# A decoder block on one Trainium2 core: the bias table read backwards, the input rows loaded before a key weight, and the row factors made one projection earlier

## The chip, the cores and the metric

The kernel is one program on one core of one Trainium2 chip. The metric is the device time of one execution in microseconds (us). TensorE (PE in the rows) multiplies, VectorE (DVE), ScalarE (ACT) and GpSimd (POOL) work on tiles, SyncE (SP) issues the transfers. PEld is TensorE's loading of weights, which overlaps its products.

## The reference

One decoder block for x of 512 tokens by 1024 channels in float32, with one batch and one layer:

```
h = rms_norm(x)
q, k, v (three branches), gates, conv inputs = h @ w_in
NSA heads (8 query heads, 2 key groups, width 64):
    logit[t, s] = q[t] . k[s] / 8 + bias[head, bucket(t - s)], causal
    branches: compressed keys (31 blocks), selected blocks, window; each softmax, gated, summed
conv heads: y = b * dwconv3(c * x~)
x1 = x + rms_norm(concat @ w_out)
y  = x1 + rms_norm(gated conv MLP(rms_norm(x1)))
```

The bias depends on the distance t - s alone, so each head has one vector of 512 numbers, and every row of the table is that vector shifted by one place.

## The kernel before

Every dense product is made of three passes in a short float32 form: each operand is split into hi and lo. For a weight tile ScalarE rounds hi (L84) and VectorE subtracts to get lo (L85); for eight weights, those of the compression's first layer (c1_0 to c1_7, shown as w_c_0 to w_c_7 in the lists below), GpSimd makes lo instead, on the same line 85. A product of a weight with h is three matmuls for each of eight k steps, 24 in all, on lines 167 (hi by hi), 168 and 169 (lo of the weight), so the lo part is first needed by the third.

Weights come through one object W, in the order of use: 512 KB each, loaded some tiles ahead into three raw buffers (L72) and split fewer tiles ahead. All transfers are issued by SP in the order of the program.

The start runs in this order on TensorE: the products of the value columns (pv, L297 to L299), then k0 and k1 (the keys of the selected and of the window branch, pp_k), c0 (the keys to compress, pp_c), q0 and q1 (queries), then c1 (the values to compress) together with the first attention part. ScalarE takes the mean square of the four row tiles of x (L307, tile xt); GpSimd makes 1/rms of it (L308, L309); VectorE puts it on a diagonal (dgs), and one product of ones and dgs (prb, L335) spreads it over the partitions; ScalarE copies it to Rb (L336). Every projection that leaves PSUM is multiplied by Rb on VectorE (L372: kt for keys, ct for what is compressed, qt for queries). Keys are then split into KK (L131, L132), queries into Q (hi L397, lo L398). ScalarE also writes the values V (L350).

What is to be compressed is laid out by `blocks`: eight additions for the keys' tile and eight for the values' tile (L417, tile x), then a split into X (L131, L132), which the first compression layer multiplies (`hidden_steps`, ph, L441).

Attention goes in parts of four heads. For each head two products make the logits (sc, L593); one VectorE instruction adds the bias table and takes the minimum of the row (L597); ScalarE takes the exponential (L599); `scale` divides by the row sums two heads at a time (L604, L606; then head 0 on GpSimd, L611, the others on ScalarE, L613). The probabilities are transposed on TensorE (tr, L622), split (pth, ptl) and multiplied with the values (o, L630, L631). Between these pieces the order of work named in ORDER fills TensorE: c1, then q2, the compression's hidden layer, q3, and the convolution heads' weights from g0 on (pcg).

The bias table U[p, h, u] holds, at row p, the vector of head h shifted by p. The vector goes to DRAM (vd, 8 by 640), is copied there 128 times (two transfers to vrows, one for four heads each), and is read back with a pitch that is one number short of the row, so that each row is shifted by one more place.

From the end of the startup on, the order on each engine is found by a scheduler, which follows the program's order but may move an instruction past others.

Of the kernel before, what the change touches and what calls it, by code (L numbers as in the profile page):

```python
"""Hybrid decoder block (NSA heads + short convolution, then a gated conv MLP) on one core.

Float32 products run as three float32r passes over operands split exactly into
hi + lo (12 + 12 significant bits): hi*hi + hi*lo + lo*hi.  The attention logits
and the P.V products keep all four parts.

With these shapes N_SEL covers every key block (n_sel = SEQ / L_SLC) and WINDOW =
SEQ, so the selected and the sliding branch both see exactly the causal keys: top-k
only permutes the blocks, and softmax does not depend on their order.
"""  # L10
# [11 lines left out]
F32 = mybir.dt.float32  # L22
# [8 lines left out]
NT = S // P          # token tiles  # L31
KT = D // P          # contraction tiles of the model width
# [9 lines left out]
# the projections and the first layer of the compression as they fill the gaps of the attention:  # L42
# values to compress c1, queries q, hidden layer h, second layer s, then gate g, input x, output gate b
ORDER = ("c1 q2:4 h0 q2:4 h1 q3:4 h2 q3:4 h3 g0:4 h4 g0:4 h5 x0:4 h6 x0:4 h7 s b0 "
         "g1 x1 b1 g2 x2 b2 g3 x3 b3")
LOADS = "T0 g w T1 T2 w b T3 T4 T5 w T6 T7", "x0 x1 v x2 x3 s0", "s1"
T_TILES = 20         # kc vc ks kw q0-3 then (c x b) x 4
WARM = 8             # products on zeros while the first loads are under way
# [6 lines left out]
class Stream:  # L55
    """The dense weights in the order of their use: loaded some tiles ahead, split fewer ahead."""

    def __init__(self, tc, nc, raw, ring, items, loads=3, splits=2):
        self.tc, self.nc, self.raw, self.ring, self.items = tc, nc, raw, ring, items
        self.loads, self.splits = loads, splits  # L60
        self.raws, self.tiles = [], []
        self.at = 0
        self.early = False     # whether the splits go before what was emitted shortly before them
        self.pool_lo = set()  # tiles whose lo part GpSimd makes
        self.pieces = {}     # tiles that are split in pieces of so many columns
        self.other = {}      # tiles that go to another pool than the ring
# [41 lines left out]
def block_kernel(ctx: ExitStack, tc: tile.TileContext, a, out):  # L108
# [20 lines left out]
    def split(hi, lo, src):  # L129
        """hi = src rounded to 12 significant bits, lo = src - hi (exact)."""  # L130
        act(hi, src, AF.Copy)  # L131
        nc.vector.tensor_tensor(lo, src, f32(hi), op=ALU.subtract)  # L132

    VK = [0, 2, 5, KT]       # the k tiles of the value columns, as they share a tile of the ring
# [27 lines left out]
    W = Stream(tc, nc, rawp, ringp, items)  # L162
# [30 lines left out]
    # the tensor engine's clock comes up while the first loads are under way  # L193
# [6 lines left out]
    # bias tables: U[p, h, u] = -(bias of distance p + 384 - u), +BIG where it is negative  # L200
    # row r of vrows is the whole of vd; reading with a pitch one short shifts it by r
# [4 lines left out]
    vrows = [dram.tile([P, 4 * 640], F32, name=f"vrows{n}") for n in range(2)]  # L206

    def load(what):
        """A name of LOADS: w the next weights, g the gains, b and v the bias (its table, then its vector),
        s rows of shifted bias, T columns and x rows of the input."""  # L210
        if what == "w":
            W.ahead(0, len(W.raws) + 1)
        elif what == "g":
            nc.sync.dma_start(gT, a["g_mix_pre"])
        elif what == "b":
            nc.sync.dma_start(oh[:NB, :S], a["onehot"])
            nc.sync.dma_start(relT, a["relT"])
        elif what == "v":
            nc.sync.dma_start(vd[:, :S], vec[:NH, :S])
            nc.sync.dma_start(vd[:, S:], vbig)  # L220
        elif what[0] == "s":
            n = int(what[1])
            nc.sync.dma_start(vrows[n], bass.AP(tensor=vd.tensor, offset=vd.offset + n * 4 * 640,
                                                ap=[[0, P], [1, 4 * 640]]))
        elif what[0] == "T":
            k = int(what[1])
            nc.sync.dma_start(xT[:, k, :], a["xT"][k * P:(k + 1) * P, :])
        else:
            t = int(what[1])
            nc.sync.dma_start(xt[:, t, :], a["x"][t * P:(t + 1) * P, :])  # L230
# [17 lines left out]
    def rstd_of(ss, name):  # L248
        """1 / rms of a row from the two halves of its mean square."""
        r = const.tile([P, 1], F32, tag="rstd", bufs=4, name=name)  # L250
        nc.gpsimd.tensor_scalar(r, ss[:, 0:1], ss[:, 1:2], EPS, op0=ALU.add, op1=ALU.add)  # L251
        nc.gpsimd.tensor_tensor(r, r, mhalf, op=ALU.pow)
        return r
# [17 lines left out]
    # The mean square of a row divides what comes out of the products, not what goes in.  # L271
    R = const.tile([P, 2, NT], F32, name="R")        # 1 / rms and its negative, by token
    Rb = ph1.tile([P, S], F32, name="Rb")            # the same, by token along the row
# [28 lines left out]
    for what in LOADS[2].split():  # L302
        load(what)

# [13 lines left out]
    def proj(name, ahead=None):  # L318
        p = mm_bank(f"pp_{name}")
        for _ in proj_steps(p, W.next(ahead)):  # L320
            pass
        return p

    W.ahead(2, 3)
    for t in range(NT):
        square1(t)
    W.ahead(3, 3)
    pk = [proj("k0", 0), proj("k1", 0)]
    pc0 = pt_bank("pp_c0")
    wq = W.next(0)  # L330
    W.ahead(1, 2)
    for _ in proj_steps(pc0, wq, 0, 3):
        pass
# [3 lines left out]
    for _ in proj_steps(pc0, wq, 3, KT):  # L337
        pass
    nc.vector.tensor_scalar(R[:, 1], R[:, 0], -1.0, None, op0=ALU.mult)
    U = r16("U").rearrange("p (h u) -> p h u", h=NH)  # L340
    for n, v in enumerate(vrows):
        nc.sync.dma_start(U[:, 4 * n:4 * n + 4, :], bass.AP(tensor=v.tensor, offset=v.offset + P - 1,
                                                            ap=[[4 * 640 - 1, P], [640, 4], [1, S]]))
# [44 lines left out]
    # queries, scaled by -1/8; even heads keep hi in the low half, odd heads in the high half  # L388
# [14 lines left out]
    # X[(l parity, d), l // 2, k/v, hi/lo, (group, block)] = kv + pe, the blocks padded to 32  # L403
# [25 lines left out]
    def hidden_steps(c):  # L429
        """First layer of the compression; rows 0-63 from X hi, rows 64-127 from X lo."""  # L430
        if c == 0:
            phs[0] = mm_bank("ph")
        w = W.next()
        for l in range(2):
            l2 = 2 * c + l
            for kv in range(2):
                xs = X[:, l2, kv].rearrange("p s g n -> p (s g n)")
                for s in range(2):
                    cc = slice(l * 512 + kv * 256, l * 512 + kv * 256 + 256)
                    # one group over the bank: its first product opens it  # L440
                    MM(phs[0][:, kv * 256:kv * 256 + 256], xs, w[:, s, cc],  # L441
                       start=l2 == 0 and kv == 0 and s == 0, stop=l2 == 15 and kv == 1 and s == 1)
            yield

    def second_layer():
        w2 = ph1.tile([P, 2, 2, HD], F32, tag="gz", bufs=1, name="w2")     # (half, k/v)
# [103 lines left out]
    def compressed_softmax(i):  # L550
# [7 lines left out]
        uv = U[:, :, u0:u0 + 16 * (nv - 1) + 1:16]  # L558
# [15 lines left out]
    class Part:  # L574
        """Four heads of a group on a tile of queries: one branch, or both for the first tile."""
# [8 lines left out]
        def score(self, r):  # L584
# [9 lines left out]
            for b in range(len(self.bs)):  # L594
                v = p[:, b * nk:(b + 1) * nk]
                m = self.mins[:, r, b:b + 1]
                nc.vector.tensor_tensor_reduce(v, sc[:, b * nk:(b + 1) * nk], U[:, h, 384 - P * i:S], 1.0, 3e38,  # L597
# [54 lines left out]
    def finish(o, i, g):  # L652
        # rows 0-63: V hi . P, rows 64-127: V lo . P
# [23 lines left out]
    for n, (i, g, bs) in enumerate(parts):  # L677
# [6 lines left out]
        # the share that goes between this part's pieces  # L684
# [45 lines left out]
    def token_major(w_tiles, ys, acts, on_half, on_tile, order):  # L730
        """The last products of a streamed contraction, one token tile after another."""
# [14 lines left out]
    with tc.tile_pool(name="ph2", bufs=1, reuse_waits="tile") as ph2:  # L746
# [49 lines left out]
        # the first tiles of the MLP in halves of the tokens, behind the norm of the last rows  # L796
# [83 lines left out]
def _bucket_onehot():  # L880
    """[bucket, 511 - distance], a constant of the shapes alone."""
# [5 lines left out]
    m[bucket, S - 1 - d] = 1.0  # L887
# [50 lines left out]
```

## Time and profile before

| what | value |
| --- | --- |
| time, median of 3 runs | 634.92 us (633.7 to 635.61) |
| span of the profiled execution | 633.9 us |
| TensorE busy | 617.5 us, 97% |
| VectorE busy | 382.2 us, 60% |
| ScalarE busy | 306.5 us, 48% |
| GpSimd busy | 62.7 us, 10% |
| mean granted TensorE clock | 0.995 |

The times are of whole executions, and the span is from the first to the last instruction of the one execution that was profiled, whose own time the page doesn't give: the median lies 1.0 us above that span, and the three runs lie within 1.9 us of each other. A row of a timeline gives the start, the duration, the engine, the line, and the tiles; `x4` joins four like instructions, and what stands in brackets is the idle time of the engine just before, with what ended it. Durations of matmuls overlap, so the pace of TensorE is read from the starts.

### The profile page before, as it was taken

The numbers are of one execution on the slowest core, as the hardware profiler recorded it, in microseconds if no ns is written. First come the engines' busy times: TensorE is split into PE (matmuls) and PEld (weight loads), VectorE is DVE, ScalarE is ACT, GpSimd is POOL, SyncE is SP. The second block draws the span as 40 slices with busy tenths as digits, with TensorE's granted clock in tenths as the row PEclk, the third lists the DMA queues.
The fourth block names the chain that finished last, engine by engine and source line by source line (L and its number), as shares of the span: only waits on it lengthen the run. The fifth ranks groups of instructions, "written<-read, shape, count | busy, mean of one in ns | idle before, by whom it ended". The sixth has DMA issues, their size and how long they took to land.

```text
span 633.9 us, 8027 instructions
## 1 busy us (share of the span) xinstructions
PE 617.5 (97%) x2980; PEld 511.3 (81%) x2980; DVE 382.2 (60%) x668; ACT 306.5 (48%) x556; POOL 62.7 (10%) x88
## 2 busy tenths in 40 slices
PE   8998899999999999999999999999999999999995
PEld 6886688887778788898888888888888888888884
DVE  5379967898988756648666656565656542222225
ACT  6546765798878644426443434444344422222212
POOL 1102453002130202200000000000000000000001
PEclk9999899999999999999999999999999999999999
DMA  8993355201121483004222233232322232232203
GB/s 293 329 304 129 133 180 189 74 10 43 42 78 53 169 280 130 8 5 143 93 96 98 99 100 101 100 100 99 101 87 95 89 114 87 94 100 99 67 0 133
DMA packets 25302, 72.00 MB, mean 114 GB/s; under 512 B 3136, under 2 KB 7048, under 8 KB 25008
## 3 DMA queue, kind: packets, MB, share of 16 engines
q1 hardware_dynamic: 25264, 71.50, 33.9%
q8 instruction: 23, 0.38, 0.2%
q14 instruction: 15, 0.12, 0.1%
HBM read 67.50 MB, written 4.74 MB: 114 GB/s over the span
## 4 chain that ended last, share of the span: by engine, by line
PE 80%; DVE 10%; DMA 3%; ACT 3%; issue 2%; POOL 1%; SPq 0%; DVEq 0%; POOLq 0%; ACTq 0%
PE pu L168 13%; PE pu L169 13%; PE pu L167 13%; PE z L743 6%; PE z L742 6%; PE z L744 6%; PE y L744 2%; PE y L743 2%; PE y L742 2%; DVE x L417 2%; DMA raw_q<-in_w_t 2%; PE tr L622 2%; PE sc L593 2%; PE o L631 1%; PE o L630 1%
## 5 line engine op out<-in xcount | busy, mean ns | idle before, releaser
L167 PE MATMUL pu<-h2T,w_u 128*128 128x512 f32 (+1 forms) x384 | 142.8, 372 | 0.0
L168 PE MATMUL pu<-h2T,w_u 128*128 128x512 f32 (+1 forms) x384 | 142.7, 372 | 0.0
L169 PE MATMUL pu<-h2T,w_u 128*128 128x512 f32 (+1 forms) x384 | 142.6, 371 | 0.0
L167 PEld LDWEIGHTS pu<-h2T,w_u 128*128 128x128 f32 x384 | 72.3, 188 | 12.6
L168 PEld LDWEIGHTS pu<-h2T,w_u 128*128 128x128 f32 x384 | 72.3, 188 | 12.6 <-DVE h2T L132 0.2
L169 PEld LDWEIGHTS pu<-h2T,w_u 128*128 128x128 f32 x384 | 72.3, 188 | 12.4
L826 DVE SCALAR_TENSOR_TENSOR cv<-pu,ffnw,cv 128x511 f32<-128x511 f32 x44 | 32.9, 749 | 70.2 <-ACT cv L825 70.2
L85 DVE TENSOR_TENSOR w_d<-raw_d,w_d 128x1024 fp32r<-128x1024 f32 x22 | 26.9, 1224 | 72.8 <-ACT w_d L84 72.8
L742 PE MATMUL z<-w_d,aT 128*128 128x512 f32 x176 | 68.5, 389 | 0.0
L743 PE MATMUL z<-w_d,aT 128*128 128x512 f32 x176 | 68.5, 389 | 0.0
L744 PE MATMUL z<-w_d,aT 128*128 128x512 f32 x176 | 68.5, 389 | 0.0
L825 ACT ACTIVATE cv<-pu,ffnw 128x512 f32<-128x512 f32 x44 | 30.3, 688 | 64.0 <-PE pu L169 63.9
L84 ACT ACTIVATE w_d<-raw_d 128x1024 fp32r<-128x1024 f32 x22 | 23.3, 1059 | 75.2 <-PE z L744 75.2
L85 DVE TENSOR_TENSOR w_u<-raw_u,w_u 128x1024 fp32r<-128x1024 f32 x44 | 53.4, 1217 | 5.9 <-ACT w_u L84 5.8
L84 ACT ACTIVATE w_u<-raw_u 128x1024 fp32r<-128x1024 f32 x44 | 46.2, 1052 | 6.6 <-PE pu L169 6.3
L599 ACT ACTIVATE P<-P,mins 128x512 f32<-128x512 f32 (+3 forms) x64 | 35.4, 554 | 11.5 <-DVE mins L597 11.1
L742 PEld LDWEIGHTS z<-w_d,aT 128*128 128x128 f32 x176 | 33.0, 188 | 6.9
L744 PEld LDWEIGHTS z<-w_d,aT 128*128 128x128 f32 x176 | 33.0, 188 | 6.9
L743 PEld LDWEIGHTS z<-w_d,aT 128*128 128x128 f32 x176 | 33.0, 188 | 6.7
L131 ACT ACTIVATE aT<-cv 128x512 fp32r<-128x512 f32 x22 | 13.9, 632 | 49.5 <-DVE cv L843 49.5
L251 POOL TENSOR_SCALAR rsz<-ssz 128x1 f32<-128x1 f32 x4 | 1.2, 300 | 355.2 <-ACT jz L865 355.2
L827 DVE SCALAR_TENSOR_TENSOR cv<-pu,ffnw,cv 128x510 f32<-128x510 f32 x44 | 32.8, 748 | 1.5
(215 smaller groups left out, 1158.7 us busy)
## 6 DMA issues: line engine op xcount, KB each, us to landing
raw_u<-in_w_u SPq DMA_DIRECT2D x44, 512.0 KB, 3.3
raw_d<-in_w_d SPq DMA_DIRECT2D x22, 512.0 KB, 3.2
raw_c<-in_w_c SPq DMA_DIRECT2D x8, 512.0 KB, 3.3
raw_o<-in_w_o SPq DMA_DIRECT2D x8, 512.0 KB, 3.4
vrows<-vd SPq DMA_DIRECT2D x2, 1280.0 KB, 10.4
xT<-in_xT SPq DMA_DIRECT2D x8, 256.0 KB, 5.3
xt<-in_x SPq DMA_DIRECT2D x4, 512.0 KB, 7.1
raw_q<-in_w_t SPq DMA_DIRECT2D x4, 512.0 KB, 7.0
```

The costliest lines, as they stand in the source:

```text
L84: self.nc.scalar.activation(t[:, 0, cs], self.raws[n][:, cs], AF.Copy)
L85: eng.tensor_tensor(t[:, 1, cs], self.raws[n][:, cs], f32(t[:, 0, cs]), op=ALU.subtract)
L167: MM(dst, wh, xh, start=first, stop=False)
L168: MM(dst, wh, xl, start=False, stop=False)
L169: MM(dst, wl, xh, start=False, stop=last)
L599: act(v, v, AF.Exp, bias=m, scale=-1.0, accum_out=self.sums[:, r, b:b + 1])
L742: MM(y, oh_, w[:, 0, cs], start=first, stop=False)
L743: MM(y, ol_, w[:, 0, cs], start=False, stop=False)
L744: MM(y, oh_, w[:, 1, cs], start=False, stop=last)
L825: act(t, pu, AF.Copy, scale=ffnw[:, m, 2:3])
L826: nc.vector.scalar_tensor_tensor(t[:, 1:], pu[:, :S - 1], ffnw[:, m, 1:2], t[:, 1:], op0=ALU.mult, op1=ALU.add)
L827: nc.vector.scalar_tensor_tensor(t[:, 2:], pu[:, :S - 2], ffnw[:, m, 0:1], t[:, 2:], op0=ALU.mult, op1=ALU.add)
```

## The change

Four edits, all in the first part of the kernel.

- The two copies to vrows are gone. The vector is written the other way round in distance, at place 127 of a row of vd, with 127 large numbers ahead of it; UR is read from vd with a pitch of one number, and the attention reads each of its rows backwards (`bias`, step -1, and step -16 for the compressed branch).
- The four row tiles of x (and the vector between them) are loaded before the second key weight k1; after them follow k1, c0 and q0.
- ScalarE's order follows from that: the squares of x stand ahead of the split of k1.
- prb and Rb are made after three of the eight k steps of k1, where they were made after three of c0's.

```diff
-LOADS = "T0 g w T1 T2 w b T3 T4 T5 w T6 T7", "x0 x1 v x2 x3 s0", "s1"
+LOADS = "T0 g w T1 T2 w b T3 T4 T5 w T6 T7 w", "x0 x1 v x2 x3 w"
...
-    W = Stream(tc, nc, rawp, ringp, items)
+    W = Stream(tc, nc, rawp, ringp, items, loads=0)
...
-            nc.sync.dma_start(vd[:, :S], vec[:NH, :S])
-            nc.sync.dma_start(vd[:, S:], vbig)
-        elif what[0] == "s":
-            n = int(what[1])
-            nc.sync.dma_start(vrows[n], bass.AP(tensor=vd.tensor, offset=vd.offset + n * 4 * 640,
-                                                ap=[[0, P], [1, 4 * 640]]))
+            nc.sync.dma_start(vd[:, P - 1:P - 1 + S], vec[:NH, :S])
+            nc.sync.dma_start(vd[:, :P - 1], vbig[:, :P - 1])
...
-    W.ahead(2, 3)
     for t in range(NT):
         square1(t)
-    W.ahead(3, 3)
-    pk = [proj("k0", 0), proj("k1", 0)]
-    pc0 = pt_bank("pp_c0")
+    W.ahead(3, 4)
+    pk = [proj("k0", 0), mm_bank("pp_k1")]
     wq = W.next(0)
-    W.ahead(1, 2)
-    for _ in proj_steps(pc0, wq, 0, 3):
+    for _ in proj_steps(pk[1], wq, 0, 3):
         pass
     prb = mm_bank("prb")
     MM(prb, ones, dgs, start=True, stop=True)
     act(Rb, prb, AF.Copy)
-    for _ in proj_steps(pc0, wq, 3, KT):
+    for _ in proj_steps(pk[1], wq, 3, KT):
+        pass
+    pc0 = pt_bank("pp_c0")
+    W.loads = 3
+    wq = W.next(0)
+    W.ahead(1, 2)
+    for _ in proj_steps(pc0, wq):
         pass
     nc.vector.tensor_scalar(R[:, 1], R[:, 0], -1.0, None, op0=ALU.mult)
-    U = r16("U").rearrange("p (h u) -> p h u", h=NH)
-    for n, v in enumerate(vrows):
-        nc.sync.dma_start(U[:, 4 * n:4 * n + 4, :], bass.AP(tensor=v.tensor, offset=v.offset + P - 1,
-                                                            ap=[[4 * 640 - 1, P], [640, 4], [1, S]]))
+    UR = r16("UR").rearrange("p (h u) -> p h u", h=NH)
+    for n in range(2):
+        nc.sync.dma_start(UR[:, 4 * n:4 * n + 4, :], bass.AP(tensor=vd.tensor, offset=vd.offset + n * 4 * 640,
+                                                             ap=[[1, P], [640, 4], [1, S]]))
+
+    def bias(h, u, n, step=1):
+
+        v = UR[:, h, S - 1 - u]
+        return bass.AP(tensor=v.tensor, offset=v.offset, ap=[*v.ap, [-step, n]])
...
-        uv = U[:, :, u0:u0 + 16 * (nv - 1) + 1:16]
+        uv = bias(slice(None), u0, nv, 16)
...
-                nc.vector.tensor_tensor_reduce(v, sc[:, b * nk:(b + 1) * nk], U[:, h, 384 - P * i:S], 1.0, 3e38,
+                nc.vector.tensor_tensor_reduce(v, sc[:, b * nk:(b + 1) * nk], bias(h, 384 - P * i, nk), 1.0, 3e38,
...
-    m[bucket, S - 1 - d] = 1.0
+    m[bucket, d] = 1.0
```

The lists below are the instructions of one engine in program order, without durations; lines of the changed kernel differ by a few. The number of matmuls is the same.

On ScalarE, before, from the split of k1 (the first row) to the split of c0 (the last), with the squares (xt, L307) and the values (V, L350) between them:

```order
L84 ACTIVATE w_k_292<-raw_k_190 128x1024
L307 ACTIVATE xt,ss_295<-xt 128x1024
L350 ACTIVATE V_139<-pv_144,R 128x4x64
L307 ACTIVATE xt,ss_300<-xt 128x1024
L350 ACTIVATE V_139<-pv_145,R 128x4x64
L307 ACTIVATE xt,ss_305<-xt 128x1024
L350 ACTIVATE V_139<-pv_146,R 128x4x64
L307 ACTIVATE xt,ss_310<-xt 128x1024
L350 ACTIVATE V_139<-pv_147,R 128x4x64
L84 ACTIVATE w_c_315<-raw_c_245 128x1024
```

The same place of the changed kernel, to the copy of Rb:

```order
L299 ACTIVATE xt,ss_290<-xt 128x1024
L299 ACTIVATE xt,ss_295<-xt 128x1024
L351 ACTIVATE V_139<-pv_144,R 128x4x64
L351 ACTIVATE V_139<-pv_145,R 128x4x64
L299 ACTIVATE xt,ss_300<-xt 128x1024
L351 ACTIVATE V_139<-pv_146,R 128x4x64
L299 ACTIVATE xt,ss_305<-xt 128x1024
L351 ACTIVATE V_139<-pv_147,R 128x4x64
L84 ACTIVATE w_k_310<-raw_k_209 128x1024
L84 ACTIVATE w_c_313<-raw_c_211 128x1024
L325 ACTIVATE Rb<-prb 128x512
```

The split of k1 has moved from ahead of the four squares to behind the last of the values, and Rb follows the split of c0 directly.

On VectorE, before, at the second half of the first attention part (the row minima L597, the row sums, and the additions x of the values to compress):

```order
L597 ISA P_585,mins_561<-sc_584,U 128x512
L597 ISA mins_561 128x1
L604 RECIPROCAL sums_560<-sums_560 128x2
L606 TENSOR_TENSOR sums_560<-sums_560,G 128x2
L85 TENSOR_TENSOR w_q_523<-raw_q_486,w_q_523 128x1024
L372 TENSOR_TENSOR ct_626<-pp_c_596,Rb 128x512
L597 ISA P_662,mins_595<-sc_661,U 128x512
L597 ISA mins_595 128x1
L417 TENSOR_TENSOR x_1_0_628<-ct_626,peT 64x8x31 x2
L604 RECIPROCAL sums_560<-sums_560 128x2
L417 TENSOR_TENSOR x_1_0_628<-ct_626,peT 64x8x31
L606 TENSOR_TENSOR sums_560<-sums_560,G 128x2
```

In the changed kernel the first attention part on VectorE, from the lo of the first two queries' heads on:

```order
L399 SCALAR_TENSOR_TENSOR Q_456<-qt_512,Q_456 64x512 x2
L85 TENSOR_TENSOR w_q_519<-raw_q_482,w_q_519 128x1024
L373 TENSOR_TENSOR qt_548<-pp_q_518,Rb 128x512
L598 ISA P_559,mins_557<-sc_558,UR 128x512
L598 ISA mins_557 128x1
L598 ISA P_565,mins_557<-sc_564,UR 128x512
L598 ISA mins_557 128x1
L399 SCALAR_TENSOR_TENSOR Q_456<-qt_548,Q_456 64x512 x2
...
L605 RECIPROCAL sums_556<-sums_556 128x2
L607 TENSOR_TENSOR sums_556<-sums_556,G 128x2
L373 TENSOR_TENSOR ct_622<-pp_c_592,Rb 128x512
L418 TENSOR_TENSOR x_1_0_624<-ct_622,peT 64x8x31 x2
```

Both pairs of row sums now stand ahead of ct and of the additions x. The lo of the second queries (qt_548) stands behind two row minima; before, both queries were split before the first of them.

On GpSimd, before, behind the last 1/rms:

```order
L611 TENSOR_SCALAR P_563<-P_563,sums_560 128x512
L85 TENSOR_TENSOR w_c_0_597<-raw_c_0_488,w_c_0_597 128x1024
L85 TENSOR_TENSOR w_c_1_643<-raw_c_1_490,w_c_1_643 128x1024
L85 TENSOR_TENSOR w_c_2_727<-raw_c_2_600,w_c_2_727 128x1024
L611 TENSOR_SCALAR P_662<-P_662,sums_594 128x512
```

and in the changed kernel:

```order
L85 TENSOR_TENSOR w_c_0_593<-raw_c_0_484,w_c_0_593 128x1024
L85 TENSOR_TENSOR w_c_1_639<-raw_c_1_486,w_c_1_639 128x1024
L612 TENSOR_SCALAR P_559<-P_559,sums_556 128x512
L85 TENSOR_TENSOR w_c_2_723<-raw_c_2_596,w_c_2_723 128x1024
```

The lo parts of the first two compression weights now come before the scaling of the first head. TensorE's order changes in the same place: before, after the fourth of the first part's logits (and q1 mixed with c1) q2 was mixed with transposes; in the changed kernel all 24 matmuls of q1 come first, then the logits of heads 0 and 1, nine matmuls of c1, the logits of head 2, one of c1, those of head 3, the other fourteen of c1, and twelve of q2. From the first matmul of g0 on, TensorE's order is the same in both.

## Rows read from the trace of the kernel before

**Rows 1.** The page: the span, and TensorE's busy time and share.
```profile
span 633.9 us, 8027 instructions
PE 617.5 (97%) x2980; PEld 511.3 (81%) x2980; DVE 382.2 (60%) x668; ACT 306.5 (48%) x556; POOL 62.7 (10%) x88
```

**Rows 2.** Busy time by stretch: length, PE, PEld, DVE, ACT, POOL, clock, DMA.
```profile
65.00:70.00 5.00, 2.40 (x7) 1.91 (x8) 4.78 (x10) 3.01 (x5) 0.43 (x1) 0.77 0.40 142
70.00:75.00 5.00, 5.00 (x29) 4.34 (x29) 4.96 (x9) 4.42 (x8) 2.11 (x1) 0.89 0.30 105
...
120.00:200.00 80.00, 78.55 (x434) 63.90 (x432) 70.27 (x220) 67.47 (x171) 13.47 (x22) 1.00 0.17 51
200.00:620.00 420.00, 419.51 (x1965) 350.10 (x1964) 218.41 (x289) 163.37 (x261) 13.58 (x23) 1.00 0.29 98
```

**Rows 3.** Timeline of TensorE: waits between 50 and 68 us, the first matmul of g0.
```profile
53.37 1.47 PE L593 MATMUL sc<-KK,Q 128*128 128x512 f32 x4 [0.93 <-issue]
...
60.54 0.33 PE L622 MATMUL tr<-ident,P 128*128 128x128 f32 x1 [0.78 <-POOL P L611]
...
67.60 0.45 PE L622 MATMUL tr<-ident,P 128*128 128x128 f32 x1 [2.96 <-ACT P L613]
...
85.48 0.40 PE L167 MATMUL pcg<-hT,w_tg 128*128 128x512 f32 x1
```

**Rows 4.** Chain of waits: the transfer of q0, then the additions and row sums.
```profile
22.99 11.78 DMA raw_q<-in_w_t
...
61.13 2.10 DVE x L417
63.24 2.55 DVE x L417
65.80 0.17 DVE sums L604
```

**Rows 5.** Timeline of ScalarE: k1's rounding, then values and squares in turn.
```profile
16.78 1.06 ACT L84 ACTIVATE w_k<-raw_k 128x1024 fp32r<-128x1024 f32 x1
...
20.79 0.47 ACT L350 ACTIVATE V<-pv,R 128x256 fp32r<-128x256 f32 x1 [1.68 <-PE pv L299]
21.17 1.05 ACT L307 ACTIVATE xt<-xt 128x1024 f32<-128x1024 f32 x1
...
23.26 0.47 ACT L350 ACTIVATE V<-pv,R 128x256 fp32r<-128x256 f32 x1 [0.95 <-POOL R L309]
```

**Rows 6.** Timeline of TensorE: the first matmul of k0, of k1 and of q1.
```profile
21.69 0.39 PE L167 MATMUL pp_k<-hT,w_k 128*128 128x512 f32 x1
...
27.15 0.39 PE L167 MATMUL pp_k<-hT,w_k 128*128 128x512 f32 x1
...
44.35 0.39 PE L167 MATMUL pp_q<-hT,w_q 128*128 128x512 f32 x1
```

**Rows 7.** Timeline of VectorE: key scaling, query lo, weight lo, additions.
```profile
37.15 1.28 DVE L372 TENSOR_TENSOR kt<-pp_k,Rb 128x512 f32<-128x512 f32 x2
...
52.58 2.84 DVE L398 SCALAR_TENSOR_TENSOR Q<-qt,Q 64x512 fp32r<-64x512 f32 x4
...
58.70 1.23 DVE L85 TENSOR_TENSOR w_q<-raw_q,w_q 128x1024 fp32r<-128x1024 f32 x1
...
66.77 2.99 DVE L417 TENSOR_TENSOR x<-ct,peT 64x248 f32<-64x248 f32 x5
```

**Rows 8.** Timeline of GpSimd: two lo parts of compression weights.
```profile
60.45 4.97 POOL L85 TENSOR_TENSOR w_c<-raw_c,w_c 128x1024 fp32r<-128x1024 f32 x2
```

**Rows 9.** VectorE's groups by form: the bias table's readers, mean ns after the busy time.
```profile
L597 DVE CUSTOM_DVE_ANT_0 P<-sc,U 128x512 f32<-128x512 f32 x16 | 10.9, 688 | 0.6 <-PE sc L593 0.4
...
L559 DVE TENSOR_TENSOR zc<-pcs,U 128x248 f32<-128x248 f32 x1 | 0.6, 592 | 1.2 <-PE pcs L547 1.2
L560 DVE TENSOR_TENSOR zc<-pcs,zc 128x248 f32<-128x248 f32 x1 | 0.4, 411 | 0.0
```

**Rows 10.** Transfers: issues, KB each, median us from issue to landing.
```profile
vrows<-vd SPq DMA_DIRECT2D x2, 1280.0 KB, 10.4
```

More of the change, by code (lines that the diff above doesn't have):

```diff
@@ L205, in block_kernel @@
     vd = dram.tile([NH, 640], F32, name="vd")
-    vrows = [dram.tile([P, 4 * 640], F32, name=f"vrows{n}") for n in range(2)]
     def load(what):
@@ L300, in block_kernel @@
     dgs = ph1.tile([P, S], F32, tag="pth", bufs=2, name="dgs")
-    for what in LOADS[2].split():
-        load(what)
     def square1(t):
```

## The prediction

> **What bounds the kernel now.** The page comes first: TensorE is busy for 617.5 of 633.9 us [rows 1]. No product is added or removed, so at most the 16.4 us in which it idles, and any time at a low clock, can be won or lost. Busy time by stretch says where they lie: from 200 to 620 us TensorE idles 0.5 us in all, from 120 to 200 us 1.45 [rows 2]. From the first matmul of g0, at 85.48 us, its order is the same in both kernels, so the question is whether that matmul comes earlier or later than 85.48 [rows 3]; the rest follows it unchanged unless the reversed reads cost VectorE something later.
>
> Before g0, the timeline of TensorE shows three waits that the change touches: 0.93 us for the queries (the lo parts of Q run up to the start of that product [rows 7]), 0.78 us for head 0's scaled probabilities, and 2.96 us for the scaled probabilities of heads 2 and 3 [rows 3]. The chain of waits tells what the first and last hang on. The first goes back to the transfer of q0, under way for 11.78 us from 22.99 on, behind the copies to vrows; it landed at 34.8 [rows 4]. The key scaling on VectorE came only at 37.15, behind the split of q0 [rows 7]. The last goes back to two additions x that took 2.10 and 2.55 us, with the row sums behind them [rows 4]; undisturbed, five take 2.99 [rows 7]. These two stand beside GpSimd's two lo parts, 4.97 us from 60.45 on [rows 8]. So a VectorE instruction that reads two tiles of SBUF is held while GpSimd makes a lo part, and the two engines alternate: one addition, one lo part. After the 2.96 us the granted clock fell, to 0.77 in 65 to 70 us and 0.89 in 70 to 75 [rows 2], that is, to 1.2 GHz for part of each. This cost (0.23 + 0.11) x 5 = 1.7 us.
>
> **The change part by part.**
>
> *Less DMA, x earlier.* Two copies of 1,280 KB go, with a median of 10.4 us to landing each [rows 10], and x moves ahead of k1. The raw weights have no queue of copies ahead of them: q0, which landed at 34.8, should land around 25. By itself this is worth nothing at its place, since TensorE runs through from 21.69 to beyond 44 us; it frees VectorE, which can scale the keys some 5 us sooner (about 32, where it was 37.15 [rows 7]). The reads of UR are issued around 30 us and first needed at 53. Even at 10.4 us each [rows 10], one behind the other, they would be there at 30 + 20.8 = 50.8: hidden.
>
> *k1's split behind the squares.* Before, ScalarE rounded k1 at 16.78, ahead of the first square [rows 5]. Now it stands behind four squares and four values. Two squares fit before 20.79, where the first value waits for its products. From there: value 1 at 21.17 (0.38 later), square 3 at 21.55, value 3 at 21.55 + 2.09 (the row distance of a square and the next value, 21.17 to 23.26 [rows 5]) = 23.64, square 4 at 24.02, value 4 at 26.11, k1 at 26.49. Rounding takes 1.06 [rows 5], lo 1.23 [rows 7]: lo is ready at 28.8. The first matmul of k1 was at 27.15 and their pace is (27.15 - 21.69) / 24 = 0.2275 us [rows 6], so the third, the first to read lo, was at 27.60. It is **1.2 us late**. That the squares themselves have their data is the early x's doing; before, the first square waited for x.
>
> *prb moved.* The same two passes at another place, so TensorE's sum is unchanged. Rb is ready some 4.5 us sooner.
>
> *The first attention part.* q1, first at 44.35 [rows 6], now at 45.55, runs unmixed for 24 x 0.2275 = 5.46 and ends at 51.0. On VectorE, key scaling and keys come first, then the additions for the keys (eight at 0.6 and two lo parts), and the first query's lo ends at about 51.05: the **0.93 wait is gone**. Next on VectorE is a weight's lo (1.23) up to 52.3, and GpSimd's first lo part, 4.97 / 2 = 2.45 [rows 8], starts there and ends at 54.75. Between them VectorE scales the second query (0.64, half of [rows 7]) and takes two row minima (0.68 each [rows 9]), which read one PSUM tile each and weren't held. The second query's lo is two instructions of 0.65 with both inputs in SBUF. The first is held to 54.75 and ends at 55.4; TensorE, with the logits of heads 0 and 1 (0.9) and nine of c1 done, is there at 51.0 + 0.9 + 9 x 0.2275 = 53.95: **1.45 us of waiting** for head 2. GpSimd then takes its second lo part, 55.2 to 57.6, and the second half of the query's lo ends at 58.2; TensorE is ready 0.7 after 55.4: **2.1 us** for head 3. Then fourteen of c1 end at 61.85. VectorE scales them to 62.9, does eight additions (0.6 each), a weight's lo and the lo of X, to 68.9. TensorE meanwhile has twelve and five of q2, a logit and some small products, and stands before the hidden layer's products on the values at 66.8: **2.1 us** more. The row sums now come ahead of the additions, so the **0.78 and 2.96 are gone**, and with them the **1.7** at the low clock.
>
> *Sum.* Out: 0.93 + 0.78 + 2.96 + 1.70 = 6.37. In: 1.2 + 1.45 + 2.1 + 2.1 = 6.85. The difference is +0.5. Counted on from the last wait instead (68.9 plus the work left before g0: 45 matmuls of 512 columns at 0.2285, 30 of the hidden layer at 0.1165, 12 transposes at 0.09, all estimates from the starts in the timeline, and 1.0 of small waits), g0 comes at 84.8, that is -0.7. I take the middle, 0.
>
> *The reversed read.* 64 row minima now read their bias with step -1. No row of before has a negative step. A step of 16 is there: L559 takes 592 ns where L560, the like with step 1, takes 411 [rows 9], that is 181 / 248 = 0.73 ns an element. Bounds: nothing, or 0.73 ns on 16 x (512 + 384 + 256 + 128) = 20,480 elements = 14.9 us of VectorE. Numbers read backwards lie next to each other as they do forwards, which is nearer to L560: I take nothing. A gain is excluded: no less is read. The Trainium skill (SBUF — State Buffer, section "Door 1: The DMA port swizzle") says that consecutive accesses to one 16-byte line run at full bandwidth and each new line costs; L559's row agrees, and by this rule step -1 is free. Its Vector Engine (DVE) Microarchitecture Reference (section "5.1 Performance modes") lists an operand with a negative step as not measured, and no run here shows one.
>
> **The rivals.**
>
> (a) *The second lo part doesn't hold the queries' lo* (it comes late, or VectorE's two instructions go through together). For it: the two are queued next to each other on VectorE, while GpSimd's second lo also needs ScalarE's rounding. Against: in [rows 4, 8] a lo part came between two additions queued just so. Then the 2.1 for head 3 is gone, and with the account that gives -0.7 the time falls by 2.8, to 632.1. The outer end has none of the three new waits near 55 to 68 us: 634.9 - 6.37 + 1.2 = 629.7. Chance 0.22, mostly near 632.3.
>
> (b) *The clock falls in the new waits.* Before, it fell after an idle time of 2.96 us [rows 2, 3]; here 1.45 and 2.1 us of waiting lie 0.7 us apart. If it falls, the 1.7 isn't won: 634.9 + 1.7 = 636.6, the side of slower or just under it. Against: the waits of 0.93 and 0.78 us cost no clock. It decides from the point where the two waits act as one. Chance 0.16.
>
> (c) *The reversed read costs as a strided one does*, 0.73 x 512 = 0.37 us a row minimum at full width. The four of the first part lie on its chain: 4 x 0.37 = 1.5 us. Of the whole 14.9 us most falls between 120 and 200 us, where VectorE has 80 - 70.27 = 9.7 us free [rows 2]; what doesn't fit, 14.9 - 9.7 = 5.2 us, bounds the loss there. Between 1.5 and 1.5 + 5.2 I take 4: 638.9. The changed trace decides: 688 or about 1,060 ns at 512 columns [rows 9]. Chance 0.07.
>
> (d) *The transfers of UR are slow* and the copies of KK and the compression's weights queue behind them. At 10.4 us each they land at 51, where the logits need KK: some 2.5 us, 637.4. Chance 0.05. Against: vrows were large copies within DRAM, these are reads of 2 KB rows of one 20 KB vector.
>
> **How the numbers follow.** The forecast, no change that can be measured, has 0.5. 0.3% of this time, 1.9 us, is about what a measurement of this kernel can tell from no change: 633.0 to 636.8. The profiled execution's span of 633.9 stands 1.0 below the median of the runs, and the differences above, worked out in that span, are laid on the median: 634.9. Its own range is 633.4 to 636.2. The whole range takes in (a) near its middle and (b), up to (d): 632.0 to 637.2, leaving out (c) and the outer end of (a). Faster: 0.20 of (a) and 0.05 of the forecast, 0.25. Slower: (c), (d) and 0.07 of (b), 0.19. Same: the rest, 0.45 + 0.02 + 0.09 = 0.56.
>
> **What would show it.** On the timeline of TensorE: k1's third matmul at 28.8 with a wait near 1.2; logits of heads 0 and 1 at 51 without a wait; waits of about 1.5 and 2.1 before heads 2 and 3, for queries; none for the probabilities; one of about 2 before the hidden layer's products; g0 between 84.8 and 86.0. On VectorE row minima of 688 ns. The clock 1.00 from 11 us to the end of that stretch. The forecast is wrong if the lo parts of GpSimd come elsewhere than beside the second query's, as the engines' alternation rests on starts that differ by tenths of a us, or if k1's transfer, now behind 2 MB of x, lands after 26.5.

## The result, and the profile after

The changed kernel takes 638.75 us, the median of 13 runs (637.02 to 642.03), against 635.61 for the kernel before in 13 runs beside it (633.7 to 638.46). The ratio is 1.006, with a 95% interval of 1.0045 to 1.0076: slower by 0.6%, some 3.8 us, where no measurable change was forecast and 637.2 was the upper end of the range. (In the experiments one execution, of e9, took 2,813.74 us at a mean granted clock of 0.212; it is left out of that kernel's time and comparison, and e12 repeats it.)

The page of the changed kernel, to [rows 1]:

```profile
span 638.0 us, 8019 instructions
PE 619.2 (97%) x2980; PEld 513.0 (80%) x2980; DVE 381.2 (60%) x668; ACT 306.7 (48%) x556; POOL 62.3 (10%) x88
```

Its busy time by stretch, with the columns of [rows 2]:

```profile
50.00:60.00 10.00, 6.66 (x28) 4.71 (x27) 8.84 (x12) 7.11 (x11) 5.17 (x2) 0.96 0.54 193
60.00:65.00 5.00, 5.00 (x17) 3.98 (x18) 1.70 (x8) 3.47 (x7) 0.70 (x1) 0.74 0.29 105
65.00:70.00 5.00, 5.00 (x26) 3.92 (x24) 4.69 (x7) 1.52 (x2) 0.00 (x0) 1.00 0.14 48
70.00:75.00 5.00, 2.93 (x12) 2.52 (x12) 4.81 (x10) 2.96 (x6) 0.60 (x1) 0.79 0.15 57
75.00:85.00 10.00, 10.00 (x55) 8.47 (x55) 6.96 (x13) 7.47 (x13) 4.90 (x3) 0.94 0.31 107
...
200.00:620.00 420.00, 419.45 (x1969) 350.34 (x1968) 219.04 (x305) 165.67 (x270) 13.53 (x24) 1.00 0.29 98
```

From 200 to 620 us nothing differs from [rows 2]; TensorE is 1.7 us longer busy with the same products. The granted clock is what tells why: from 50 to 85 us it fell twice, where the kernel before has one fall. Worked out as the prediction did for [rows 2], 0.04 x 10 + 0.26 x 5 = 1.7 us went with the first and 0.21 x 5 + 0.06 x 10 = 1.65 with the second.

The timeline of TensorE in the changed kernel (the first matmul of k0, then every wait up to the first matmul of g0, and some matmuls at the low clock):

```profile
22.74 0.39 PE L167 MATMUL pp_k<-hT,w_k 128*128 128x512 f32 x1
...
28.62 0.50 PE L167 MATMUL pp_k<-hT,w_k 128*128 128x512 f32 x1 [0.26 <-ACT w_k L84]
...
29.88 0.50 PE L169 MATMUL pp_k<-hT,w_k 128*128 128x512 f32 x1 [0.53 <-DVE w_k L85]
...
52.19 1.17 PE L594 MATMUL sc<-KK,Q 128*128 128x512 f32 x4
...
56.98 0.73 PE L594 MATMUL sc<-KK,Q 128*128 128x512 f32 x2 [1.54 <-DVE Q L399]
...
59.75 1.22 PE L594 MATMUL sc<-KK,Q 128*128 128x512 f32 x2 [1.81 <-DVE Q L399]
60.77 0.63 PE L168 MATMUL pp_c<-hT,w_c 128*128 128x512 f32 x1
61.20 0.63 PE L169 MATMUL pp_c<-hT,w_c 128*128 128x512 f32 x1
...
72.11 1.06 PE L442 MATMUL ph<-w_c,X 128*128 128x256 f32 x6 [2.07 <-DVE X L132]
...
88.47 0.50 PE L632 MATMUL o<-ptl,V 128*128 128x512 f32 x1 [0.39 <-DVE ptl L132]
...
89.76 0.40 PE L167 MATMUL pcg<-hT,w_tg 128*128 128x512 f32 x1
```

The waits stand where the prediction put them: at k1 (two short ones, for hi and for lo, where it had one), none ahead of heads 0 and 1, then 1.54, 1.81 and 2.07 us; the three of [rows 3] are gone. After the wait before head 3 the matmuls start 0.43 us apart (60.77 and 61.20), where 0.2275 is their pace: 1.2 GHz, not 2.4. After the one before the hidden layer the granted clock is low again (0.79 from 70 to 75 us).

The first k0 comes at 22.74 us, at 21.69 in [rows 6]. The products ahead of it are the same in both, and the profiles of one and the same kernel differ there (21.69 and 21.08 for the kernel before; 22.74, 20.81 and 21.13 for the changed one). In this profile of the changed kernel the clock also fell in the start, by 0.17 x 10 = 1.7 us, which e8 and e11 don't show (1.00 there). From 10 to 20 us, in the changed kernel and then in the one before:

```profile
10.00:20.00 10.00, 10.00 (x64) 9.70 (x64) 6.93 (x10) 7.32 (x12) 1.54 (x4) 0.83 1.03 401
```

```profile
10.00:20.00 10.00, 10.00 (x73) 9.23 (x72) 7.83 (x9) 7.98 (x12) 0.71 (x2) 1.00 1.00 386
```

So what a kernel does before g0 is read here from the first k0 to the first g0: 85.48 - 21.69 = 63.79 us before, 89.76 - 22.74 = 67.02 now, and behind g0 the two spans differ by 0.2 us (633.9 - 85.48 = 548.4, 638.0 - 89.76 = 548.2). All of the difference lies between these two matmuls or ahead of them.

On VectorE and GpSimd, the wait before head 3 in the changed kernel:

```profile
55.92 3.77 DVE L399 SCALAR_TENSOR_TENSOR Q<-qt,Q 64x512 fp32r<-64x512 f32 x2
...
53.98 5.17 POOL L85 TENSOR_TENSOR w_c<-raw_c,w_c 128x1024 fp32r<-128x1024 f32 x2 [26.88 <-ACT w_c L84]
```

Two instructions that take 1.40 us by themselves (e2) took 3.77 beside GpSimd's two lo parts. ScalarE had rounded both of these weights ahead of the second query:

```profile
52.84 2.19 ACT L84 ACTIVATE w_c<-raw_c 128x1024 fp32r<-128x1024 f32 x2
54.94 1.26 ACT L398 ACTIVATE Q<-qt 64x512 fp32r<-64x512 f32 x2
```

And VectorE's groups by form, for the reversed read:

```profile
L598 DVE CUSTOM_DVE_ANT_0 P<-sc,UR 128x512 f32<-128x512 f32 x16 | 10.9, 688 | 0.8 <-PE sc L594 0.6
...
L560 DVE TENSOR_TENSOR zc<-pcs,UR 128x248 f32<-128x248 f32 x1 | 0.6, 609 | 1.3 <-PE pcs L548 1.3
...
L561 DVE TENSOR_TENSOR zc<-pcs,zc 128x248 f32<-128x248 f32 x1 | 0.4, 412 | 0.0
```

A row minimum takes 688 ns backwards as it did forwards [rows 9]; the step of -16 costs 609 ns against 592 for 16.

### The profile page after: what moved, and what is told of

It reads as the page before. It is cut to its first block, busy times and chain, and to the rows that moved or that the text cites. A ratio compares the mean times of both kernels' runs of the same rounds, so it can differ in the third digit from the quotient of the medians.

```text
span 638.0 us, 8019 instructions
## 1 busy us (share of the span) xinstructions
PE 619.2 (97%) x2980; PEld 513.0 (80%) x2980; DVE 381.2 (60%) x668; ACT 306.7 (48%) x556; POOL 62.3 (10%) x88
## 4 chain that ended last, share of the span: by engine, by line
PE 79%; DVE 5%; ACT 2%; issue 1%; DMA 0%; POOL 0%; DVEq 0%; POOLq 0%; ACTq 0%
PE pu L168 13%; PE pu L167 13%; PE pu L169 13%; PE z L743 6%; PE z L745 6%; PE z L744 6%; PE y L745 2%; PE y L744 2%; PE y L743 2%; PE sc L594 2%; PE tr L623 2%; PE o L632 1%; PE o L631 1%; PE ph L442 1%; PE pcg L167 1%
## 5 line engine op out<-in xcount | busy, mean ns | idle before, releaser
L594 PE MATMUL sc<-KK,Q 128*128 128x256 f32 (+2 forms) x112 | 30.0, 356 | 3.9 <-DVE Q L399 3.3
```

The lines of the kernel that those rows point to most:

```text
L594: MM(sc[:, :n], q, k, start=s == 0, stop=s == 1)
```

## The experiments

The theory after the result (theory A): the waits cost what was forecast, and the clock falls after them, where the forecast had no fall. Its rivals (theory B, put anew for each run): the loss comes from the start of the kernel, or from x ahead of k1 as a whole, and the waits are hidden or would be there anyway. e5 then asks whether it is the place of k1's split on ScalarE (theory C) or the order of the transfers (theory D).

**e1.** 14 products of no use fill the waits before heads 2 and 3.

```diff
+            for _ in range({2: 6, 3: 8}.get(r, 0) if self.n == "300" else 0):
+                MM(sc, hT[:, 0, 0, :P], hT[:, 0, 0, :], start=True, stop=True)
             for s in range(2):
...
     for r in range(4):
+        if r == 2:
+            fill(3)
         cur.score(r)
...
-    done = 0
+    done = 3
```

> The changed kernel with 14 products of no use (six ahead of the logits of head 2, eight ahead of those of head 3, written to the bank that the logits then overwrite), and one matmul of c1 moved behind head 3. Theory A (the clock falls because TensorE idles 1.54 and 1.81 us there, and that costs another 1.7): the waits are filled, the granted clock is 1.00 from 60 to 65 us, and the time falls by 1.2 to 1.7, to about 637.2, though work was added. Theory B (the loss comes from the start of the kernel, and the clock's fall at 60 us does not hang on this idle time): the clock falls all the same, and the time is that of the changed kernel, 638.7, or a little above.

637.89 us; ratio to the kernel before 1.0028 (1.0007 to 1.0048), 0.3% below the changed kernel's 1.006 although it does more (the two intervals just touch). The busy time by stretch of e1:

```profile
60.00:65.00 5.00, 5.00 (x23) 4.13 (x22) 2.65 (x8) 4.42 (x8) 0.70 (x1) 1.00 0.31 105
...
70.00:75.00 5.00, 4.28 (x16) 3.66 (x17) 2.70 (x6) 2.99 (x6) 1.93 (x1) 0.66 0.00 0
```

The fall at 60 us is gone, the one behind the hidden layer's wait (1.88 us here, not filled) is there. This agrees with theory A, but as e8 lacks the first fall without any filling, this one profile doesn't show that the filling prevented it. The runs do: each has its mean granted clock on record, and one minus that clock, times the span, is what the clock cost in it from the first to the last instruction (idle time at a low clock counted in). This is 2.8 us on average over the 12 runs of e1 and 4.9 over the 13 of the changed kernel: 2.1 us less with the waits filled, more than one fall; the start, where a fall can come too, is the same in both.

**e2.** The two lo parts that held the second query, on VectorE.

```diff
-    W.pool_lo |= {f"c1_{c}" for c in range(8)}
+    W.pool_lo |= {f"c1_{c}" for c in range(2, 8)}
```

> The changed kernel with the lo parts of the first two compression weights made by VectorE in place of GpSimd. Theory A (GpSimd's lo parts hold the queries' lo parts, and the idle time then lowers the clock): the two instructions of the second query's lo take 1.4 us together, not 3.77; head 3 starts at about 57.9 rather than 59.75; no low clock at 60 us; VectorE has 2.4 us more to do, so the wait for the hidden layer stays near 2. Together 2 to 3.5 us less: 635.2 to 636.8. Theory B: the lo parts only change places, 638.7.

634.45 us; ratio 0.9973 (0.9955 to 0.9991). The timeline of VectorE and of TensorE in e2:

```profile
55.42 1.40 DVE L399 SCALAR_TENSOR_TENSOR Q<-qt,Q 64x512 fp32r<-64x512 f32 x2
...
56.16 1.14 PE L594 MATMUL sc<-KK,Q 128*128 128x512 f32 x2 [1.85 <-DVE Q L399]
...
68.29 0.98 PE L442 MATMUL ph<-w_c,X 128*128 128x256 f32 x6 [1.60 <-DVE X L132]
```

The hold is gone (1.40 for 3.77), and with it the wait before head 3, and the gain is a little more than expected. The wait before head 2 grew to 1.85, since a weight's lo now stands ahead of the query's on VectorE, and one fall came behind it, which theory A had not expected. k1 comes as late as in the changed kernel (waits of 0.26 and 0.53 us), and yet the loss is gone.

**e3 and e4.** Parts of the change: the backward table alone, and everything but x ahead of k1. e3 is the kernel before with the diff's lines on vd, vrows, U and the onehot. e4 is the changed kernel with

```diff
-LOADS = "T0 g w T1 T2 w b T3 T4 T5 w T6 T7 w", "x0 x1 v x2 x3 w"
+LOADS = "T0 g w T1 T2 w b T3 T4 T5 w T6 T7 w w", "x0 x1 v x2 x3"
...
+    W.ahead(2, 3)
     for t in range(NT):
         square1(t)
```

> The kernel before with the table read backwards alone: no copies to vrows, k1 ahead of x and Rb within c0 as before. Theory A: the weights come early all the same, so the scheduler's order of the first attention part is that of the changed kernel, with waits before heads 2 and 3 and a low clock after them, but without the 1.2 us at k1: 637.5. Theory B (x ahead of k1 is the loss): 635.0 to 636.0, as before or a little less.

> The changed kernel with k1 loaded and split ahead of x again; the backward table and Rb within k1 stay. Theory A: k1 loses its waits, 1.2 us; the waits before heads 2 and 3 and the low clocks stay: 637.5. Theory B (x ahead of k1 and its split behind the squares is the whole loss): 635.0 to 636.0.

e3: 635.01 us, ratio 0.998 (0.9958 to 1.0001). e4: 634.48 us, ratio 0.9985 (0.9963 to 1.0007). Theory A expected 637.5 of each and was wrong: without x ahead of k1 the whole loss is gone, not 1.2 us of it. In both profiles the wait before head 2 is 1.06 us, that before head 3 is gone, that before the hidden layer is 2.87, and the clock doesn't fall between 20 and 120 us. The timeline of TensorE in e4:

```profile
54.08 0.72 PE L595 MATMUL sc<-KK,Q 128*128 128x512 f32 x2 [1.06 <-DVE Q L400]
...
65.45 0.98 PE L443 MATMUL ph<-w_c,X 128*128 128x256 f32 x6 [2.87 <-DVE X L132]
```

Over their 12 runs each, though, the clock cost 3.2 us (e3) and 3.1 (e4), as much as in the 88 runs of the kernel before that stand beside the experiments (3.2): most of these runs had a fall somewhere, which can't be placed from a mean. So the table read backwards is worth at most a little, and Rb within k1 nothing that can be told from e3.

**e5.** Is it the transfers' order, or the place of k1's split? x stays ahead of k1; the split goes between the second and the third square.

```diff
     for t in range(NT):
+        if t == 2:
+            W.ahead(2, 3)
         square1(t)
```

> The changed kernel, x loaded ahead of k1 as there, with the split of k1 put between the second and the third square on ScalarE. Theory C (the place of k1's split on ScalarE, behind four squares and four values, is what x ahead of k1 costs): no wait at k1, the scheduler's order as with k1 first, 634.0 to 635.5. Theory D (the order of the transfers itself costs): 637.5 to 638.7.

634.99 us, ratio 0.9997 (0.9978 to 1.0016): theory C. The timeline of TensorE, and of GpSimd, VectorE and ScalarE about the second query, in e5:

```profile
53.69 0.74 PE L596 MATMUL sc<-KK,Q 128*128 128x512 f32 x2 [1.06 <-DVE Q L401]
66.39 0.98 PE L444 MATMUL ph<-w_c,X 128*128 128x256 f32 x6 [3.40 <-DVE X L132]
...
50.60 2.48 POOL L85 TENSOR_TENSOR w_c<-raw_c,w_c 128x1024 fp32r<-128x1024 f32 x1 [25.87 <-ACT w_c L84]
55.33 2.40 POOL L85 TENSOR_TENSOR w_c<-raw_c,w_c 128x1024 fp32r<-128x1024 f32 x1 [2.24 <-ACT w_c L84]
...
52.68 1.67 DVE L401 SCALAR_TENSOR_TENSOR Q<-qt,Q 64x512 fp32r<-64x512 f32 x2
...
54.21 1.04 ACT L84 ACTIVATE w_c<-raw_c 128x1024 fp32r<-128x1024 f32 x1
```

With k1 in time the scheduler rounds the second compression weight only at 54.21, behind the exponentials of heads 0 and 1; in the changed kernel both are rounded ahead of the second query, and GpSimd makes both lo parts in one run. Here the second lo part starts at 55.33, when the query's lo is done: rival (a) of the prediction, in another kernel. The query's lo takes 1.67 us, not 3.77.

**e7, e8, e11.** The kernel before once more, and the changed kernel twice more, unedited.

> The kernel before, unchanged, profiled a second time. If the clock's fall belongs to a kernel's waits: waits of 0.93, 0.78 and 2.96 again and one fall after the last. If it differs from execution to execution: the same waits, and a fall or none; the start of k0 (21.69) may differ too by up to 2 us, as in the other profiles.

> The changed kernel, unchanged, profiled a second time. If the falls belong to the waits: 1.5, 1.8 and 2.1 us again, with falls at 60 and 72 us. If they differ from execution to execution: the same waits with none, one or two falls, and a span between 634.5 and 640.

> The changed kernel a third time, for the clock alone: the same waits (1.5, 1.8 and 2.1 us, 0.1 either way), and one or two falls of the clock after them; first g0 behind first k0 by 65.6 us with one fall, by 67.0 with two, by 63.9 with none.

Busy time by stretch of e8, and then of e11:

```profile
50.00:60.00 10.00, 6.72 (x28) 4.71 (x27) 8.94 (x15) 7.09 (x14) 5.56 (x3) 1.00 0.48 161
60.00:65.00 5.00, 5.00 (x25) 4.18 (x24) 3.43 (x7) 2.88 (x5) 0.38 (x1) 1.00 0.00 0
65.00:70.00 5.00, 2.93 (x18) 2.27 (x17) 4.74 (x10) 1.75 (x4) 0.00 (x0) 0.96 0.28 105
70.00:75.00 5.00, 5.00 (x23) 4.20 (x22) 2.78 (x9) 4.01 (x7) 2.91 (x2) 0.70 0.12 23
```

```profile
50.00:60.00 10.00, 6.70 (x25) 4.66 (x24) 8.96 (x15) 6.67 (x12) 5.25 (x2) 0.87 0.50 170
60.00:65.00 5.00, 5.00 (x15) 3.90 (x14) 0.70 (x7) 2.74 (x6) 0.69 (x1) 0.57 0.02 9
65.00:70.00 5.00, 4.91 (x25) 3.81 (x23) 4.75 (x8) 1.61 (x3) 0.00 (x0) 1.00 0.16 44
```

The waits are the same to 0.05 us (1.49, 1.79, 2.07 in e8; 1.49, 1.81, 2.03 in e11). In e8 the clock falls only behind the last and costs (0.04 + 0.30) x 5 = 1.7 us; in e11 it falls behind the second for twice as long and costs 0.13 x 10 + 0.43 x 5 = 3.45, and doesn't fall behind the last. So the falls differ from execution to execution with the waits unchanged: 3.35, 1.7 and 3.45 us. The kernel before lost 1.7 again, behind a wait of 2.93 (e7; its other two waits were 0.50 and 0.77, for 0.93 and 0.78).

**e6.** e4, with the third query weight ahead of the hidden layer.

```diff
-ORDER = ("c1 q2:4 h0 q2:4 h1 q3:4 h2 q3:4 h3 g0:4 h4 g0:4 h5 x0:4 h6 x0:4 h7 s b0 "
+ORDER = ("c1 q2:8 h0 h1 q3:4 h2 q3:4 h3 g0:4 h4 g0:4 h5 x0:4 h6 x0:4 h7 s b0 "
```

> The kernel with k1 ahead of x (e4), and the third query weight's products all ahead of the hidden layer's first products, so that TensorE has 2.3 us of other work while VectorE lays out the values. If the wait for X (2.87 us in e4) is what remains: it falls to about 0.6, first g0 some 2.2 us earlier, 632.3. If it only moves (to the probabilities, or to the second query): 634.5, as e4.

634.43 us, ratio 0.9983 (0.9968 to 0.9998): as e4. The timeline of TensorE shows where the 2.87 went:

```profile
65.52 0.97 PE L443 MATMUL ph<-w_c,X 128*128 128x256 f32 x6 [0.42 <-DVE X L132]
69.19 0.51 PE L633 MATMUL o<-ptl,V 128*128 128x512 f32 x1 [0.37 <-DVE ptl L132]
73.99 0.49 PE L632 MATMUL o<-pth,V 128*128 128x512 f32 x1 [0.86 <-ACT pth L131]
...
76.05 0.50 PE L633 MATMUL o<-ptl,V 128*128 128x512 f32 x1 [1.56 <-DVE ptl L132]
```

It moved to the split probabilities, and this profile has a fall behind them.

**e9, e10, e12.** e9 and e12 are e4 with e2's edit, e10 is that with the order of e6.

> e4 and e2 together: k1 ahead of x, and the lo parts of the first two compression weights on VectorE. If the two costs are separate (k1's lateness; the held lo of the second query): no wait at k1, the wait before head 2 at 1.1 or more (VectorE makes a weight's lo ahead of it), none before head 3, about 2.5 to 4 before the hidden layer, since VectorE has 2.4 us more to do: 633.5 to 634.5. If VectorE's added work cancels it: 634.5 to 635.5.

> e9 with the order of e6 (the third query weight ahead of the hidden layer). If each removes a wait of its own: waits of less than 2 us in all between 50 and 85 us, first g0 60.5 us behind the first k0 (62.0 in e4), no fall of the clock, 632.5 to 633.5. If the waits move on to the transposes' lo parts, as in e6: 634.0 to 634.5.

> e9 once more, for a profile that can be read: waits of about 1.1 before head 3, 0.8 before the first transposes, 0.7 before the hidden layer, no clock fall between the first k0 and the first g0, which lie 60.1 us apart (63.6 in the kernel before); time 632.3 again, 0.5% below the kernel before. If e9's gain was chance: 633.5 to 634.5.

e9: 631.27 us (the median of five runs), ratio 0.994 (0.9917 to 0.9962). e10: 631.7, ratio 0.9947 (0.9928 to 0.9966). e12: 633.1, ratio 0.9957 (0.9936 to 0.9978). The intervals overlap, so the order of e6 adds nothing that can be told. All three are below the kernel before and the changed one. The timeline of TensorE in e12, every wait from the first k0 to the first g0:

```profile
20.95 0.39 PE L167 MATMUL pp_k<-hT,w_k 128*128 128x512 f32 x1
...
55.24 0.70 PE L595 MATMUL sc<-KK,Q 128*128 128x512 f32 x2 [1.09 <-DVE mins L599]
...
62.71 0.33 PE L624 MATMUL tr<-ident,P 128*128 128x128 f32 x1 [0.82 <-ACT P L615]
...
65.48 0.97 PE L443 MATMUL ph<-w_c,X 128*128 128x256 f32 x6 [0.66 <-DVE X L132]
...
79.79 0.50 PE L633 MATMUL o<-ptl,V 128*128 128x512 f32 x1 [0.37 <-DVE ptl L132]
...
81.08 0.40 PE L167 MATMUL pcg<-hT,w_tg 128*128 128x512 f32 x1
```

The two costs are separate: no wait above 1.1 us is left, and no fall. Over all runs the clock cost 1.3 us in e9, 1.6 in e10 and 1.4 in e12, the least of all kernels here; as much, 0.8 to 2.1 us, goes with a last fall behind 625 us in each of the other profiles.

All profiles side by side, from the first k0 to the first g0 (us). Idle is the sum of the waits in the timeline, clock what the granted clock below 1.00 in the stretches costs, rest what is left; of e1 3.2 us of added products are taken off the rest. Where the clock falls before a wait is over, as in the changed kernel (0.04 x 10 us lost before 60 us, head 3 at 59.75), some tenths count as idle and as clock.

| kernel | k0 to g0 | idle | clock | rest |
| --- | --- | --- | --- | --- |
| before | 63.79 | 5.09 | 1.7 | 57.0 |
| before, e7 | 63.35 | 4.60 | 1.7 | 57.0 |
| changed | 67.02 | 6.60 | 3.35 | 57.1 |
| changed, e8 | 65.61 | 6.53 | 1.7 | 57.4 |
| changed, e11 | 67.07 | 6.69 | 3.45 | 56.9 |
| e1, waits filled | 65.97 | 3.46 | 1.7 | 57.6 |
| e2, lo on VectorE | 63.95 | 4.96 | 1.7 | 57.3 |
| e3, table alone | 62.11 | 4.65 | 0 | 57.5 |
| e4, k1 first | 61.97 | 4.64 | 0 | 57.3 |
| e5, k1 between | 63.30 | 4.85 | 1.7 | 56.8 |
| e6, queries first | 63.23 | 4.25 | 1.7 | 57.3 |
| e10, all three | 60.72 | 3.27 | 0 | 57.5 |
| e12, e2 with e4 | 60.13 | 2.94 | 0 | 57.2 |

The rest is the same within 0.9 us in all of them: what differs is idle time, and 1.7 us for each fall. e9's own profile, with the clock at 1.00 up to 120 us, has 60.14 from k0 to g0 as well.

## Why the prediction was wrong

The step that failed is in the sum, its last term of what goes out: "and with them the 1.7 at the low clock". The 2.96 us wait did go, but the clock fell again behind the new ones, in all three profiles of the changed kernel, for 3.35, 1.7 and 3.45 us, 2.8 on average, where the sum had 0. Against the 1.7 of the kernel before, that is 1.1 lost where 1.7 was to be won, 2.8 us in all. With it, the first account (+0.5) becomes +3.3; the profiles give 3.0 (66.57 on average for 63.57, k0 to g0), and the runs 3.8, with 2.9 to 4.8 in the interval. The runs' own clocks bear this out beyond five profiles: the clock cost 4.9 us on average in the 13 runs of the changed kernel (mean 0.9924) and 3.2 in 88 of the kernel before (0.9949), 1.6 us more where 1.7 less was forecast. With the idle time of the table, 6.61 for 4.85 on average, 1.76 more, that is 3.4 of the 3.6 us between the means of the 13 runs each (639.33 and 635.70).

- **k1's split behind the squares: right.** The third matmul of k1 stands 29.88 - 22.74 = 7.14 us behind the first of k0, before 27.60 - 21.69 = 5.91: 1.23 for 1.2. With the three waits below the terms of what comes in are 6.65 us, for 6.85.
- **The first attention part: right in place and size.** 1.54, 1.81 and 2.07 for 1.45, 2.1 and 2.1; the three old waits gone. That it is GpSimd's lo parts that hold the query's lo is shown by e2 (1.40 for 3.77). The Trainium skill (SBUF — State Buffer, section "Who interferes with whom") says that a VectorE instruction with two inputs in SBUF contends with a GpSimd one that reads SBUF, and that the order of issue decides which of them is held; the trace agrees: the query's lo, begun at 55.92 us, ended at 59.69, behind the end of the two lo parts at 53.98 + 5.17 = 59.15.
- **Reversed read and UR: right**, at 688 ns, and UR, issued at 31.37 us with a median of 9.6 to landing, was there long before the first row minimum at 54.59; rivals (c) and (d) fall.
- **The second account, -0.7, misled.** It counted the work from the hidden layer's wait to g0 at the full clock, 15.9 us. In e8, with one fall in that stretch, it took 86.42 - 68.77 = 17.65, the same 15.9 and the 1.7; and the hidden layer began 68.77 - 20.81 = 47.96 us behind the first k0, for 68.9 - 21.69 = 47.21. As both accounts shared the wrong term, their middle could not correct it.
- **Rival (b) was the nearest**, at 0.16, and too small in size. It set the fall at the first two waits taken together and left the third, the one before the hidden layer, out; and it only took the gain of 1.7 away and had no second fall.
- **What the change's parts are worth: not foreseen.** The sum had k1's lateness at 1.2 us. e4 and e5 show that with k1 split in time the whole loss is gone, since the waits before head 3 and at k1 and the scheduler's order (both compression weights rounded ahead of the second query) follow from it. e2 takes the loss away with k1 still late, so the larger part is what follows from the order, not k1's 1.2 us. Why the scheduler turns on that, and not on another's start, was not tried.

Open is what decides whether a wait is followed by a fall. Waits of 2.87 us in e3 and e4 were not, one of 1.85 in e2 was, and the same waits of one kernel were and were not (e8, e11). The chance is only counted here: where a fall comes is seen in few profiles, and the runs' mean clocks give its cost alone.

## What to carry to other kernels

A wait on TensorE can have two prices, its length and (here) 1.7 us if the clock falls behind it: don't count the second as won while waits of a like length stay or come in the new order, and give each of them a share of it. When an instruction moves on an in-order engine (here one split behind four squares), look up which order the scheduler then chooses for its followers: the place of a single rounding decided whether two engines met on the same tiles. Compare the parts of a change from one fixed matmul to another, as the start alone can differ by 2 us or more between executions.

## What the runs showed of the hardware

The fall of the clock is not fixed by the kernel: with waits equal to 0.05 us, three executions lost 3.35, 1.7 and 3.45 us to it, always about a multiple of 1.7. The start differs as well: in the profiles of all these kernels the first k0 comes between 20.76 us (e5, e6) and 24.71 (e9; 20.95 in e12, the same kernel), with the same products ahead of it. A read with step -1 costs VectorE nothing: 688 ns for 512 numbers in both directions.
